# Float32 matmuls of the attention, the scan and the merge, tied together by dependencies

## The chip, the core and the metric

The kernel runs on one core of a Trainium2 chip. The time is that of the device in microseconds (us), from one launch, on data that lies in HBM before it starts. All operands and results are float32.

## The reference, cut to what matters

A decoder block on 256 tokens of width 1024. Two branches read the same normed input: attention with 8 heads of 128 channels (with 256 tokens the block choice leaves plain causal attention), and a state-space branch (S5), a complex diagonal scan over 256 steps with 32 groups of 64 states. The branches are merged by sigmoid gates, and an MLP follows.

```python
h = rms_norm(x, norm_mix_g)
q, k, v, u, g = split(h @ w_in)                  # 3 x 1024, 512, 2 x 1024 columns
o_a = attention(rotary(q), rotary(k), v)         # softmax(q k / sqrt(128), causal) v
o_b = s5_branch(u, ...)                          # y = gelu(C scan(A, B u) + d u); val * sigmoid(gt)
x = x + (sigmoid(g_a) * o_a + sigmoid(g_b) * o_b) @ w_out
h = rms_norm(x, norm_mlp_g)
x = x + square(relu(h @ w_up)) @ w_down
return rms_norm(x, norm_final_g)
```

## The kernel before, in words

**Matmuls.** There are two kinds on TensorE. The large projections are done in float32r: a weight tile of 512 KB is loaded by a DMA on SP's queue, `split` (L82) makes a rounded high part on ScalarE (L83) and the rest on VectorE (L84), and each product is three matmuls, high by high, high by low, low by high (`mm3`, L87 to L90, with 256 moving columns; `tok_mm`, L265 to L269, with 512). The small products inside the branches are plain float32 matmuls, which the profile counts as two passes each, or transposes, one pass each:

- scores of a head, L307 and L310, with two bf16 matmuls that add the causal mask (L309, L312)
- transposes of the probabilities of a head, three at L330, copied to SBUF by ScalarE (L332)
- outputs of a head, L340 and L342, two heads into one PSUM tile `o`, which VectorE reads with the gate into `mixA` (L344)
- the scan: inputs at L539 (weights on 64 rows of the array), and the outputs `y` of a quarter: two matmuls by `Dt` on the whole array (L568) and eight on half the columns of the array, four from `sr` and four from `si` (L574). VectorE makes `sr` at L558 to L560 and `si` at L561 to L563.
- the merge after the gated linear unit: four transposes of a group, two for each half of the tokens (L662).

**Stages.** First `u` and the norm, then the projections `v`, and the four head pairs (q and k at `K`, scores at `S`, the gate at `G`, outputs at `A`) and the four scan quarters (tables `T`, scan `Q`), in the program order of the string `ORDER` (L45). Then the gated linear unit in four groups (L645 to L666), the output projection, the up and the down projection.

**Who sets the order.** The program order is not the order on an engine. A planner goes through the instructions with a simulated clock of its own and puts on each engine, at each moment, the ready instruction of the best priority. Priority is program order, and work inside `tc.high_priority` is moved ahead: the weight splits by 800 places, the scores (`S`) and the transposes and outputs (`A`) by 300 (`ATT_PRIO`). Each engine then runs its list in order, and an instruction whose inputs are late holds all behind it. Tiles come from pools with a fixed number of buffers, and a tile waits until an old one is free: two PSUM banks for scores, transposes, `o` and the merge (`att_bank`, L64), one for `y` (L565), one `sr` and one `si`, two `pr` and `pts`.

The helper `behind` (L95) adds an order without a wait between instructions of one engine. Functions that the change touches, and their callers:

Of the kernel before, what the change touches and what calls it, by code (L numbers as in the profile page):

```python
# [12 lines left out]
AF = mybir.ActivationFunctionType  # L13
ALU = mybir.AluOpType
PSUM = bass.MemoryType.PSUM

P = 128
# [31 lines left out]
def build(ctx, tc, dr, out):  # L49
# [14 lines left out]
    def att_bank(name):  # L64
        return bank("att", 2, name)
# [29 lines left out]
    def behind(ins, others, reason="table set"):  # L95
        for o in others:
            tc.add_manual_dep(ins, o.name, mybir.DependencyInfo(
                mybir.DependencyClass.NoSync, mybir.DependencyReason.DATA), reason=reason)

    def use_set(func):  # L100
        load = S.preload_act_table(func).ins
# [200 lines left out]
    scale = P ** -0.5  # L302
    mixA = p1.tile([P, KD, T], F32, name="mixA")

    def attn_head(q, k, j):
        s = att_bank("s").rearrange("p a b -> p (a b)")
        PE.matmul(s[:, 0:128], q[:, j, 0:128], k[:, j, 0:128], start=True, stop=False,  # L307
                  skip_group_check=True)
        PE.matmul(s[:, 0:128], ident_b, tri_b, start=False, stop=True, skip_group_check=True)  # L309
        PE.matmul(s[:, 128:384], q[:, j, 128:256], k[:, j, :], start=True, stop=False,  # L310
                  skip_group_check=True)
        PE.matmul(s[:, 256:384], ident_b, tri_b, start=False, stop=True, skip_group_check=True)  # L312
        st = p1.tile([P, 6], F32, tag="st", bufs=2, name="st")
        V.tensor_reduce(st[:, 0:1], s[:, 0:128], axis=mybir.AxisListType.X, op=ALU.max)
        V.tensor_reduce(st[:, 1:2], s[:, 128:384], axis=mybir.AxisListType.X, op=ALU.max)
        V.tensor_scalar(st[:, 0:2], st[:, 0:2], -scale, None, op0=ALU.mult)
        pr = p1.tile([P, 384], F32, tag="pr", bufs=2, name="pr")
        act(pr[:, 0:128], s[:, 0:128], AF.Exp, bias=st[:, 0:1], scale=scale,
                     accum_out=st[:, 2:3])
        act(pr[:, 128:384], s[:, 128:384], AF.Exp, bias=st[:, 1:2], scale=scale,  # L320
                     accum_out=st[:, 3:4])
        V.reciprocal(st[:, 4:6], st[:, 2:4])
        S.activation(pr[:, 0:128], pr[:, 0:128], AF.Copy, scale=st[:, 4:5])
        S.activation(pr[:, 128:384], pr[:, 128:384], AF.Copy, scale=st[:, 5:6])
        return pr

    def attn_pt(pr):
        pt = att_bank("pt").rearrange("p a b -> p (a b)")
        for i in range(3):
            PE.transpose(pt[:, i * P : (i + 1) * P], pr[:, i * P : (i + 1) * P], ident)  # L330
        pts = p1.tile([P, 384], F32, tag="pts", bufs=2, name="pts")
        S.copy(pts, pt[:, 0:384])  # L332
        return pts

    def attn_out(hp, prs, tha):
        pts = [attn_pt(x) for x in prs]
        o = att_bank("o")
        for j in range(2):
            hd = 2 * hp + j
            PE.matmul(o[:, j, :], v[:, 0, hd * P : (hd + 1) * P], pts[j][:, 0:256],  # L340
                      start=True, stop=False, skip_group_check=True)
            PE.matmul(o[:, j, 128:256], v[:, 1, hd * P : (hd + 1) * P], pts[j][:, 256:384],  # L342
                      start=False, stop=True, skip_group_check=True)
        V.scalar_tensor_tensor(mixA[:, 2 * hp : 2 * hp + 2, :], tha, 1.0, o,  # L344
                               op0=ALU.add, op1=ALU.mult)

    def gate(first, dst):
        acc = proj_pair(first, "g")
# [181 lines left out]
    def ssm_quad(m):  # L530
# [29 lines left out]
        V.tensor_sub(sr, sr, w)  # L560
        V.tensor_mul(si, b, sn)  # L561
        V.tensor_mul(w, d, cs)
        V.tensor_add(si, si, w)  # L563
        Wr, nWi, Dt = ssm[1:4]
        y = bank("y", 1, "y")  # L565
        for h in range(2):
            p = 2 * m + h
            PE.matmul(y[:, h, 0:P], Dt[:, p, :], U2[:, p, 1 : P + 1], start=(h == 0), stop=False,  # L568
                      skip_group_check=True)
        for i, (w_, s_) in enumerate(((Wr, sr), (nWi, si))):  # L570
            for h in range(2):
                for j in range(2):
                    q = 2 * h + j
                    PE.matmul(y[64 * j : 64 * (j + 1), h, 0:P], w_[:, 4 * m + q, :], s_[:, q, :],  # L574
                              start=False, stop=(i == 1), skip_group_check=True)
        if m < 3:
            S.copy(ysb[:, m], y[:, :, 0:P])
        for q in range(4):
# [66 lines left out]
    for q in range(4):  # L645
        acc = wide_banks(f"glu{q}") if q % 2 else [flat(mm_bank(f"glu{q}{h}")) for h in range(2)]
        for kk_ in range(2):
            wh, wl = w_unit(dr["w_glu"][2 * q + kk_], f"glu{q}{kk_}")
            for k2 in range(2):
                k, w = 2 * kk_ + k2, slice(k2 * 512, (k2 + 1) * 512)  # L650
                for hf in range(2):
                    tok_mm(acc[hf], wh[:, w], wl[:, w], yhl[0][:, 0:4], yhl[0][:, 4:8], k, hf,
                           k == 0, k == 3)
        tp = att_bank(f"mt{q}")
        for hf in range(2):
            sg = p1.tile([P, T], F32, tag=f"ab{hf}", name="sg")
            act(sg, acc[hf][:, 256:512], AF.Tanh, scale=0.5)
            V.scalar_tensor_tensor(sg, sg, 1.0, acc[hf][:, 0:256], op0=ALU.add, op1=ALU.mult)
            tb = thb[q][:, hf, :]
            V.scalar_tensor_tensor(tb, tb, 1.0, sg, op0=ALU.add, op1=ALU.mult)  # L660
            for i in range(2):
                PE.transpose(tp[:, i, hf * P : (hf + 1) * P], tb[:, i * P : (i + 1) * P], ident)  # L662
        two = slice(2 * q, 2 * q + 2)
        V.scalar_tensor_tensor(mixA[:, two, :], tp, 0.5, mixA[:, two, :],
                               op0=ALU.mult, op1=ALU.add)
# [217 lines left out]
```

## Time and profile before

| what | value |
|---|---|
| median of 3 runs | 397.01 us (397.00, 397.01, 402.53) |
| the profiled execution | 397.22 us, its span 395.4 us |
| mean granted TensorE clock | 0.997 of 2.4 GHz |
| ScalarE (ACT) busy | 225.7 us, 57% of the span |
| HBM read, and the rate over the span | 69.18 MB, 178 GB/s |

The span runs from the first to the last instruction on the core, and the time of an execution holds a little more, 1.8 us here. Times of rows are counted from the start of the span. PE is TensorE's matmuls, DVE is VectorE, ACT is ScalarE. A matmul's own duration runs on past the start of the next one, since they are pipelined, so what a matmul costs is read from start to start.

### The profile page before, as it was taken

Reading aid. Unit: us, or ns where it says so; the run is one execution under the profiler, and the core shown is the slowest. Engines: PE = TensorE matmul, PEld = TensorE weight load, DVE = VectorE, ACT = ScalarE, POOL = GpSimd, SP = SyncE. Lnnn points to the kernel's source line nnn. Section 1 sums busy time; section 2 is a strip of 40 time slices with the busy share of each in tenths; the row PEclk is TensorE's granted clock in tenths of the full one; section 3 lists DMA queues with packets and bytes.
Section 4 is the critical chain, followed back from the end, with each engine's and each line's share of the span. In section 5 each row is a group of like instructions: output and inputs, shape, how many; then the busy total and the mean of one; then the engine's idle time right before and its main releaser. Section 6 shows DMA issues by size and latency. Waiting matters only on the chain.

```text
span 395.4 us, 6719 instructions
## 1 busy us (share of the span) xinstructions
PE 385.0 (97%) x2563; PEld 344.5 (87%) x2563; DVE 293.0 (74%) x521; ACT 225.7 (57%) x360; POOL 30.9 (8%) x39
## 2 busy tenths in 40 slices
PE   7999999999999999999999999999999999999993
PEld 4988898989899797888889999999999888888883
DVE  3999999999999997559748686676676444563434
ACT  5867886674466675955636755655556334354313
POOL 4242393000000000000000000000000000000000
PEclk9999999999999999999999999999999999999998
DMA  7995843344625354346486387556565566565202
GB/s 213 389 337 188 251 165 106 108 159 143 220 93 168 107 159 163 111 159 222 153 300 229 109 269 209 180 195 208 179 202 196 183 208 184 188 213 176 92 2 106
DMA packets 23199, 71.57 MB, mean 181 GB/s; under 512 B 2944, under 2 KB 5248, under 8 KB 23168
## 3 DMA queue, kind: packets, MB, share of 16 engines
q1 hardware_dynamic: 20144, 68.92, 53.1%
q10 hardware_dynamic: 3024, 2.23, 1.9%
q8 instruction: 20, 0.33, 0.3%
q14 instruction: 11, 0.09, 0.1%
HBM read 69.18 MB, written 1.05 MB: 178 GB/s over the span
## 4 chain that ended last, share of the span: by engine, by line
PE 86%; DVE 7%; DMA 2%; POOL 1%; issue 1%; ACT 1%; SPq 0%; ACTq 0%
PE up L88 7%; PE up L89 7%; PE up L90 7%; PE dn L736 6%; PE dn L734 6%; PE dn L735 5%; PE u_acc L181 3%; PE gb L269 2%; PE gb L267 2%; PE gb L268 2%; PE glu L269 2%; PE glu L267 2%; PE glu L268 2%; PE wo L268 2%; PE wo L269 2%; PE wo L267 2%
## 5 line engine op out<-in xcount | busy, mean ns | idle before, releaser
L89 PE MATMUL up<-x2l,hi_up 128*128 128x256 f32 x256 | 70.7, 277 | 0.0
L90 PE MATMUL up<-x2h,lo_up 128*128 128x256 f32 x256 | 70.5, 276 | 0.0
L88 PE MATMUL up<-x2h,hi_up 128*128 128x256 f32 x256 | 70.1, 276 | 0.0
L84 DVE TENSOR_TENSOR lo_dn<-raw_dn,hi_dn 128x1024 fp32r<-128x1024 f32 x32 | 39.2, 1225 | 40.4 <-ACT hi_dn L83 40.4
L83 ACT CAST hi_dn<-raw_dn 128x1024 fp32r<-128x1024 f32 x32 | 33.6, 1050 | 49.1 <-PE dn L736 24.6
L84 DVE TENSOR_TENSOR lo_up<-raw_up,hi_up 128x1024 fp32r<-128x1024 f32 x32 | 38.8, 1224 | 23.5 <-ACT hi_up L83 23.5
L83 ACT CAST hi_up<-raw_up 128x1024 fp32r<-128x1024 f32 x32 | 33.3, 1049 | 35.0 <-PE up L89 16.3
L89 PEld LDWEIGHTS up<-x2l,hi_up 128*128 128x128 f32 x256 | 48.1, 188 | 0.0
L90 PEld LDWEIGHTS up<-x2h,lo_up 128*128 128x128 f32 x256 | 48.1, 188 | 0.0
L88 PEld LDWEIGHTS up<-x2h,hi_up 128*128 128x128 f32 x256 | 47.8, 188 | 0.1
L735 PE MATMUL dn<-lo_dn,hh 128*128 128x512 f32 x96 | 37.4, 389 | 0.0
L736 PE MATMUL dn<-hi_dn,hl 128*128 128x512 f32 x96 | 37.4, 389 | 0.0
L734 PE MATMUL dn<-hi_dn,hh 128*128 128x512 f32 x96 | 37.4, 389 | 0.0
L736 PEld LDWEIGHTS dn<-hi_dn,hl 128*128 128x128 f32 x96 | 18.0, 188 | 3.7
L735 PEld LDWEIGHTS dn<-lo_dn,hh 128*128 128x128 f32 x96 | 18.0, 188 | 3.7
L734 PEld LDWEIGHTS dn<-hi_dn,hh 128*128 128x128 f32 x96 | 18.0, 188 | 3.7
L89 PE MATMUL g<-xgl,hi_g 128*128 128x256 f32 x64 | 18.5, 289 | 0.0
L88 PE MATMUL k<-xgh,hi_k 128*128 128x256 f32 x64 | 18.1, 282 | 0.0
L90 PE MATMUL q<-xgh,lo_q 128*128 128x256 f32 x64 | 18.1, 282 | 0.0
L90 PE MATMUL g<-xgh,lo_g 128*128 128x256 f32 x64 | 18.1, 282 | 0.0
L88 PE MATMUL g<-xgh,hi_g 128*128 128x256 f32 x64 | 18.0, 281 | 0.0
L89 PE MATMUL q<-xgl,hi_q 128*128 128x256 f32 x64 | 18.0, 281 | 0.0
(274 smaller groups left out, 1019.6 us busy)
## 6 DMA issues: line engine op xcount, KB each, us to landing
raw_up<-w_up SPq DMA_DIRECT2D x32, 512.0 KB, 4.3
raw_dn<-w_down SPq DMA_DIRECT2D x32, 512.0 KB, 4.3
raw_v<-w_in SPq DMA_DIRECT2D x8, 512.0 KB, 5.5
raw_q<-w_in SPq DMA_DIRECT2D x8, 512.0 KB, 3.3
raw_k<-w_in SPq DMA_DIRECT2D x8, 512.0 KB, 3.2
raw_g<-w_in SPq DMA_DIRECT2D x8, 512.0 KB, 3.8
raw_gb<-w_in SPq DMA_DIRECT2D x8, 512.0 KB, 4.3
raw_glu<-w_glu SPq DMA_DIRECT2D x8, 512.0 KB, 3.3
```

Of the source, the lines that this page charges most:

```text
L83: ins = S.copy(hi, x).ins
L84: V.tensor_sub(lo, x, hi.bitcast(F32))
L88: PE.matmul(o, wh, xh, start=first, stop=False, **kw)
L89: PE.matmul(o, wh, xl, start=False, stop=False, **kw)
L90: PE.matmul(o, wl, xh, start=False, stop=last, **kw)
L181: PE.matmul(u_acc[:, m // 2, m % 2, :], w[:, ws[m]], x[:, k, :], start=(k == 0 and i == 0 and m % 2 == 0), stop=(k == KD - 1 and i == 2), ...
L267: PE.matmul(acc, xh[:, k, rows], wh, start=first, stop=False)
L268: PE.matmul(acc, xh[:, k, rows], wl, start=False, stop=False)
L269: PE.matmul(acc, xl[:, k, rows], wh, start=False, stop=last)
L734: PE.matmul(acc, xh, wh[:, w], start=(k == lead), stop=False, skip_group_check=True)
L735: PE.matmul(acc, xh, wl[:, w], start=False, stop=False, skip_group_check=True)
L736: PE.matmul(acc, xl, wh[:, w], start=False, stop=(k == end), skip_group_check=True)
```

## The change

A second helper, `after`, adds a dependency with a wait. It is used at five places. The first score matmul of a head waits for the VectorE instruction that last read the outputs of the pair before (`left`, L344). The transposes of both heads of a pair wait until the second head's probabilities are scaled (`scaled`, L324). The first output matmul of each head waits for the copies of both heads' transposes (`copied`, L332). All ten `y` matmuls of a scan quarter, the two by `Dt` and the four of `sr` among them, wait for the last VectorE instruction that makes `si` (`done`, L563). The four transposes of a merge group are issued after both halves are merged, and wait for the second half's merge (`merged`, L660). No instruction of an engine is added or taken away other than waits, and what each computes is unchanged.

```diff
+    def after(ins, others, reason):
+        for o in others:
+            tc.add_manual_dep(ins, o.name, mybir.DependencyInfo(
+                mybir.DependencyClass.Sync, mybir.DependencyReason.DATA), reason=reason)
...
+    left, scaled = [], []
     def attn_head(q, k, j):
         s = att_bank("s").rearrange("p a b -> p (a b)")
-        PE.matmul(s[:, 0:128], q[:, j, 0:128], k[:, j, 0:128], start=True, stop=False,
-                  skip_group_check=True)
+        after(PE.matmul(s[:, 0:128], q[:, j, 0:128], k[:, j, 0:128], start=True, stop=False,
+                         skip_group_check=True).ins, left[-1:], "a pair's scores together")
...
-        S.activation(pr[:, 128:384], pr[:, 128:384], AF.Copy, scale=st[:, 5:6])
+        scaled.append(S.activation(pr[:, 128:384], pr[:, 128:384], AF.Copy, scale=st[:, 5:6]).ins)
         return pr
-    def attn_pt(pr):
+    def attn_pt(pr, last):
         pt = att_bank("pt").rearrange("p a b -> p (a b)")
         for i in range(3):
-            PE.transpose(pt[:, i * P : (i + 1) * P], pr[:, i * P : (i + 1) * P], ident)
+            after(PE.transpose(pt[:, i * P : (i + 1) * P], pr[:, i * P : (i + 1) * P], ident).ins,
+                   [last], "a pair's transposes together")
         pts = p1.tile([P, 384], F32, tag="pts", bufs=2, name="pts")
-        S.copy(pts, pt[:, 0:384])
+        copied.append(S.copy(pts, pt[:, 0:384]).ins)
         return pts
+    copied = []
     def attn_out(hp, prs, tha):
-        pts = [attn_pt(x) for x in prs]
+        last = scaled[2 * hp + 1]
+        pts = [attn_pt(x, last) for x in prs]
         o = att_bank("o")
         for j in range(2):
             hd = 2 * hp + j
-            PE.matmul(o[:, j, :], v[:, 0, hd * P : (hd + 1) * P], pts[j][:, 0:256],
-                      start=True, stop=False, skip_group_check=True)
+            after(PE.matmul(o[:, j, :], v[:, 0, hd * P : (hd + 1) * P], pts[j][:, 0:256],
+                             start=True, stop=False, skip_group_check=True).ins,
+                   copied[-1:], "a pair's outputs together")
...
-        V.scalar_tensor_tensor(mixA[:, 2 * hp : 2 * hp + 2, :], tha, 1.0, o,
-                               op0=ALU.add, op1=ALU.mult)
+        left.append(V.scalar_tensor_tensor(mixA[:, 2 * hp : 2 * hp + 2, :], tha, 1.0, o,
+                                           op0=ALU.add, op1=ALU.mult).ins)
...
-        V.tensor_add(si, si, w)
+        done = V.tensor_add(si, si, w).ins
...
-            PE.matmul(y[:, h, 0:P], Dt[:, p, :], U2[:, p, 1 : P + 1], start=(h == 0), stop=False,
-                      skip_group_check=True)
+            after(PE.matmul(y[:, h, 0:P], Dt[:, p, :], U2[:, p, 1 : P + 1], start=(h == 0),
+                             stop=False, skip_group_check=True).ins, [done], "y together")
...
-                    PE.matmul(y[64 * j : 64 * (j + 1), h, 0:P], w_[:, 4 * m + q, :], s_[:, q, :],
-                              start=False, stop=(i == 1), skip_group_check=True)
+                    after(PE.matmul(y[64 * j : 64 * (j + 1), h, 0:P], w_[:, 4 * m + q, :],
+                                     s_[:, q, :], start=False, stop=(i == 1),
+                                     skip_group_check=True).ins, [done], "y together")
...
+        tbs = []
         for hf in range(2):
...
-            V.scalar_tensor_tensor(tb, tb, 1.0, sg, op0=ALU.add, op1=ALU.mult)
+            merged = V.scalar_tensor_tensor(tb, tb, 1.0, sg, op0=ALU.add, op1=ALU.mult).ins
+            tbs.append(tb)
+        for hf in range(2):
             for i in range(2):
-                PE.transpose(tp[:, i, hf * P : (hf + 1) * P], tb[:, i * P : (i + 1) * P], ident)
+                after(PE.transpose(tp[:, i, hf * P : (hf + 1) * P],
+                                    tbs[hf][:, i * P : (i + 1) * P], ident).ins,
+                       [merged], "a group's transposes together")
```

## Rows read from the trace of the kernel before

**Rows 1.** The page: busy time, share, instructions; then the last chain by engine.

```profile
PE 385.0 (97%) x2563; PEld 344.5 (87%) x2563; DVE 293.0 (74%) x521; ACT 225.7 (57%) x360; POOL 30.9 (8%) x39
...
PE 86%; DVE 7%; DMA 2%; POOL 1%; issue 1%; ACT 1%; SPq 0%; ACTq 0%
```

**Rows 2.** Windows: stretch, length; PE, PEld, DVE, ACT, POOL busy us (instructions); clock, DMA.

```profile
66.00:90.00 24.00, 23.44 (x202) 21.77 (x202) 24.00 (x47) 16.41 (x29) 0.00 (x0) 1.00 0.37 121
```

**Rows 3.** Waits of TensorE: waiting line, releaser, us in total, times, longest.

```profile
PE s L307 <- DVE k L299: 0.7, 1, 0.7
...
PE pt L330 <- ACT pr L323: 0.5, 1, 0.5
```

**Rows 4.** Timeline of TensorE, one transpose among float32r matmuls: start, us, what.

```profile
119.84 0.28 PE L88 MATMUL g<-xgh,hi_g 128*128 128x256 f32 x1
119.96 0.27 PE L330 MATMUL pt<-cst,pr 128*128 128x128 f32 x1
119.99 0.36 PE L89 MATMUL g<-xgl,hi_g 128*128 128x256 f32 x1
120.19 0.28 PE L90 MATMUL g<-xgh,lo_g 128*128 128x256 f32 x1
```

**Rows 5.** Timeline of TensorE, half of a scan quarter's outputs among float32r matmuls.

```profile
89.34 0.28 PE L90 MATMUL k<-xgh,lo_k 128*128 128x256 f32 x1
89.55 0.66 PE L574 MATMUL y<-si,nWi 128*64 128x128 f32 x8
90.14 0.38 PE L88 MATMUL k<-xgh,hi_k 128*128 128x256 f32 x1
90.36 0.28 PE L89 MATMUL k<-xgl,hi_k 128*128 128x256 f32 x1
```

**Rows 6.** Timeline of TensorE, the other places of L574 and what splits them.

```profile
82.70 0.44 PE L574 MATMUL y<-sr,Wr 128*64 128x128 f32 x4
83.07 0.44 PE L330 MATMUL pt<-cst,pr 128*128 128x128 f32 x2
83.44 0.44 PE L574 MATMUL y<-sr,Wr 128*64 128x128 f32 x4
...
103.29 0.28 PE L90 MATMUL k<-xgh,lo_k 128*128 128x256 f32 x1
103.50 0.48 PE L539 MATMUL x<-U,W 64*128 64x128 f32 x2
103.91 0.66 PE L574 MATMUL y<-si,nWi 128*64 128x128 f32 x8
104.50 1.16 PE L539 MATMUL x<-U,W 64*128 64x128 f32 x14
...
105.81 0.28 PE L89 MATMUL q<-xgl,hi_q 128*128 128x256 f32 x1
...
148.65 0.43 PE L574 MATMUL y<-sr,Wr 128*64 128x128 f32 x2
...
153.41 0.66 PE L574 MATMUL y<-si,nWi 128*64 128x128 f32 x8
```

**Rows 7.** Timeline of TensorE, a stall at transposes, and later attention work.

```profile
79.63 0.33 PE L330 MATMUL pt<-cst,pr 128*128 128x128 f32 x1 [0.49 <-ACT pr L323]
...
82.50 0.27 PE L330 MATMUL pt<-cst,pr 128*128 128x128 f32 x1
...
154.00 0.49 PE L307 MATMUL s<-k,q 128*128 128x128 f32 x2
```

**Rows 8.** Timeline of ACT: the second head's scaling of the first pair.

```profile
81.33 0.50 ACT L324 ACTIVATE pr<-pr,st 128x256 f32<-128x256 f32 x1
```

**Rows 9.** Timeline of DVE: the end of `si` twice, and a pair's outputs.

```profile
87.97 0.68 DVE L563 TENSOR_TENSOR si<-si,sw__748 128x512 f32<-128x512 f32 x1
...
149.63 0.67 DVE L563 TENSOR_TENSOR si<-si,sw__1854 128x512 f32<-128x512 f32 x1
150.23 0.67 DVE L344 SCALAR_TENSOR_TENSOR mixA<-tha,o 128x512 f32<-128x512 f32 x1
```

## The prediction, made before the changed kernel was run

> **What bounds the kernel now.** I read the busy times of the page first, then the chain that ended last, the windows of the attention stage, the list of TensorE's waits, and at the end TensorE's timeline around each small float32 product. TensorE's matmuls cover 97% of the span, and 86% of the last chain is TensorE's [rows 1]. The 97% overstates how well it is used, since a matmul's recorded time runs into the next one, but it says that TensorE hardly ever stands still. VectorE is the other full engine in the stage that the change touches: 24.00 of 24 us from 66 to 90 us, with TensorE at 23.44 [rows 2]. Yet TensorE waited for it or for ScalarE only twice in this stage, 0.7 us for the first pair's keys and 0.5 us for the first pair's probabilities [rows 3]. So time saved on TensorE's list of work is time saved at the end, as long as the other two still deliver before TensorE asks. The change adds and removes no work on any engine. It only moves instructions on TensorE's list, and so its price is in the seams between kinds of matmul and in waits.
>
> **A seam at the full array costs nothing.** Take one transpose alone among float32r matmuls [rows 4]. From the start of the L88 before it to the start of the second matmul after it is 120.19 - 119.84 = 0.35 us, which holds that L88, the transpose and one L89. A float32r matmul of this shape is 0.12 us from start to start (119.84 to 119.96), so the transpose is charged 0.35 - 0.24 = 0.11 us. Its neighbour looks slow (119.99 to 120.19 is 0.20 us) only because the transpose looks short (0.03 us). In the middle of a run a pass of this size also takes 0.11 us, since even two transposes with a tiled product before and behind them take no more than 83.44 - 83.07 = 0.37 us [rows 6]: 0.22 for the two and 0.15 at the borders of the tiled product. So gathering transposes (L330, L662), scores (L307, L310) and attention outputs (L340, L342), all full array, is worth 0.00 to 0.01 us for each seam removed. I count 19 such seams less (ten of transposes, four of outputs, two of scores, three of the merge): 0 to 0.2 us, taken as 0.1.
>
> **A seam at the tiled products costs 0.35 us.** The eight L574 matmuls of a quarter use half of the array's columns. One visit of eight passes [rows 5]: from the L90 before (89.34) to the second matmul after it (90.36) is 1.02 us, less 0.23 for the two float32r matmuls gives 0.79 us. Inside, eight passes take 90.14 - 89.55 = 0.59 us and four take 83.07 - 82.70 = 0.37 us [rows 5, 6], so two passes more cost 0.11 us. Four times 0.11 is work; the other 0.35 us is the seam, paid once for each visit whatever its length.
>
> The Trainium skill (TensorEngine Tiling (Array Packing), Key Properties) says that a change of tiling mode, not just of tile, drains TensorE. By that rule, too, only the L574 part of this change can gain, and the change from L568 to L574 inside the new block drains once as before; a reading in which each float32 visit costs something has no support there. The trace agrees with it: 0.35 us at the tiled seam against 0.01 at the other.
>
> **The sum of the y blocks.** Now the eight matmuls, 16 passes, of each quarter come in pieces: I count ten over the four quarters, six of them in [rows 5, 6], the others like them. The first quarter has three (82.70 and 83.44, split by transposes, and 89.55), the last three, the others two each. After the change there are four, one per quarter: six seams less, 6 x 0.35 = 2.1 us. Two of the ten pieces lie inside the input matmuls L539, which are tiled another way. The whole stretch there is 105.81 - 103.29 = 2.52 us, less 0.23 is 2.29 [rows 6]. L539 alone, 16 passes, would take 8 x 0.11 + 0.35 = 1.23 and L574 alone 0.79, together 2.02; the nesting costs 0.2 to 0.3 more. If the block lies clear of L539, two of these go: 0.4 us. L568's four passes cost 0.11 us each wherever they stand. From the y blocks thus 2.5 us; the bounds are 0 (every block is broken again) and 2.7.
>
> **The stall at the first transposes.** TensorE stood 0.49 us at 79.63 until the first head's probabilities were scaled [rows 7]. After the change these transposes stand behind the second head's scaling, which ended at 81.33 + 0.50 = 81.83, where the first of the second head's transposes ran at 82.50, 0.67 us later [rows 7, 8]. So the stall goes, 0.5 us. It can come back in the new place, since the saved time itself brings TensorE there 0.5 us earlier and leaves 0.2 us of the 0.67. Bounds: gain 0.5, nothing, or a wait of 0.5 as now; I take the gain. The 0.7 us stall at the keys is before any of the new waits and stays. It could grow by 0.4 us, because two seams of the first quarter's L568 that fill time before it move away; the planner puts other matmuls there, so I take 0.
>
> **The new waits.** Each waits for the same engine that the instruction waited for already, only for a later instruction of it, so I count no wait instructions. Behind each stands all of TensorE's list. The cover is that TensorE comes late to these places now. The last part of `si` ended at 88.65 and 150.30 [rows 9], and TensorE came to the matmuls that need it at 89.55 and 153.41 [rows 5, 6], 0.9 and 3.1 us later. The pair's outputs were read at 150.23 + 0.67 = 150.90 [rows 9], and the second head's scores of the next pair began at 154.00 [rows 7], 3.1 us later. The first head's scores now wait for the same read, but the second head's need not wait for a later bank any more, so the pair ends no later. What comes later is `y` itself, by about 1 us in each quarter (L568 and the `sr` half now stand in front of the `si` half): its copy on ScalarE and, for three quarters, the 24 small DMAs on ScalarE's queue, none needed before the gelu; and the next quarter's `sr`, which has one buffer and so waits for the block on VectorE. If this cover is gone, a place costs what such waits cost now, 0.5 to 0.7 us [rows 3]. SP's weight loads and POOL are not passed by anything; I put them at 0.
>
> **What the dependency does not do.** Work of the attention has 300 places of priority and may still break into a y block. It did so in two of the eight half-blocks (82.70 to 83.44 and at 148.65) [rows 6]. I take one break in the four new blocks: -0.35 us.
>
> **The sum.** 2.5 + 0.1 + 0.5 - 0.35 = 2.75 us, off the profiled execution's 397.22 us: 394.5. The profile was 0.2 us over the median of the runs, so 394.3 us for the median; forecast, **394.3 us**, 0.7% less.
>
> **Rival 1: no visible gain.** The attention breaks the blocks again: six breaks at 0.35 us eat 2.1 of the 2.5 us, the stall at the transposes stays, 397.0 - 0.5 = 396.5 us. For it: two breaks out of eight halves now. Against: a block lasts only some 1.7 us, and the wait makes its ten matmuls ready at one moment.
>
> **Rival 2: slower, the held blocks stall TensorE.** Fifteen blocks of the attention and the scan now begin with a wait (three pairs' scores, four of transposes, four of outputs, four y). The planner's clock is not the chip's; where VectorE, full from 66 to 90 us [rows 2], or ScalarE is later than planned, the whole list of TensorE stands, at 0.6 us a place. It decides from the sixth late block on (6 x 0.6 = 3.6 over the gain of 2.75 to 3.1). With ten of fifteen: 397.0 - 2.75 + 6.0 = 400.3 us. For it: both waits of now are of this kind [rows 3], and a gain brings TensorE earlier everywhere. Against: the slack of 0.67 to 3.1 us above.
>
> **Rival 3: every float32 visit costs.** If the 0.20 us after a transpose were a price of its own, 0.09 us over a matmul, the 19 full-array seams would be worth 1.7 us, 392.6 us. Against it stand [rows 4], which give the time back in the transpose.
>
> **How the numbers follow.** Chances: forecast 0.55, rival 1 0.22, rival 2 0.17, rival 3 0.06. The forecast's own bounds are 393.5 (no break, and the nesting and seams at their highest) to 395.5 (two more breaks, one late block). For 8 in 10 the range goes down to rival 3 and up through rival 1 to the mild half of rival 2, where eight blocks are late: 392.2 to 398.4. Two per cent, about what a measurement of this kernel can tell from no change, is 7.9 us. Faster than 389.1 would need more than all seams and stalls together (2.7 + 0.2 + 1.2 = 4.1): 0.01. Slower than 405.0 needs 18 late blocks of 0.6 us, more than there are, or one long one: 0.03. Within: 0.96.
>
> **What would show it.** In the timeline after: four pieces of L574, each of 16 passes with L568's four in front; a whole block, from the last float32r matmul before to the second after it, less two, at 4 x 0.11 + 8 x 0.11 + 0.35 = 1.67 us; transposes in sixes, scores of both heads side by side; no wait of 0.49 us at L330; TensorE's list of waits with nothing new over 0.7 us; and the first L734 of the down projection some 2.5 us earlier. Wrong would be: blocks still in more than six pieces (rival 1), new entries of L307, L330, L340 or L568 in the waits that sum to more than 3 us (rival 2), or a gain that lies where only transposes were gathered, after 165 us (rival 3).

## The result, and the profile after

The kernel takes **408.18 us** after the change (median of 6 runs, 406.88 to 409.02) against 397.0 us before (median of 6). One of those six runs took 402.53 us and the others 396.1 to 398.4, so versions are compared by their medians. The ratio is 1.027, 95% interval 1.024 to 1.030: slower, by four times the gain that was forecast and outside the range. The profiled execution took 408.04 us, its span is 406.2 us, 10.8 more than before.

First the page of the changed kernel: busy times, TensorE, ScalarE and the granted clock in 40 slices of 10.2 us, and the chain by engine.

```profile
PE 385.4 (95%) x2563; PEld 346.2 (85%) x2563; DVE 292.6 (72%) x521; ACT 225.9 (56%) x360; POOL 29.3 (7%) x39
...
PE   7999999999999989389999999999999999999993
...
ACT  6867977565564374644554675556555433453323
...
PEclk8999999999999999779999999999999999999998
...
PE 70%; DVE 14%; ACT 5%; issue 4%; DMA 4%; POOL 2%; ACTq 1%; SPq 0%; DVEq 0%
```

The work is the same as in [rows 1], TensorE's busy time within 0.4 us. Nearly all of the loss is in one place: the 17th slice (162.5 to 172.6 us) has a 3 for TensorE, and the clock falls to 7 in it and in the next. Stages bear that out. From the first scores to the first matmul of the gated linear unit (`glu`, L272) took 165.66 - 66.08 = 99.6 us before and 175.11 - 65.77 = 109.3 us after, 9.8 more; `glu` to output projection took 1.1 more; all later stages together are within 0.3 us.

TensorE's waits of the changed kernel (line, releaser, us in total, times, longest); this answers [rows 3].

```profile
PE pt L337 <- ACT pr L331: 8.7, 2, 8.3
PE gb L272 <- ACT thb L112: 1.4, 1, 1.4
...
PE s L314 <- ACT cs L534: 0.8, 1, 0.8
PE gb L272 <- DVE q L302: 0.7, 1, 0.7
```

One wait of 8.3 us for the scaling of probabilities is nearly all of it. TensorE's timeline after: the first pair's transposes, a whole `y` block, and the big wait.

```profile
82.62 0.88 PE L337 MATMUL pt<-cst,pr 128*128 128x128 f32 x6 [0.38 <-ACT pr L331]
...
108.92 0.28 PE L90 MATMUL q<-xgh,lo_q 128*128 128x256 f32 x1
109.04 0.61 PE L580 MATMUL y<-U,Dt 128*128 128x128 f32 x4
109.58 0.66 PE L586 MATMUL y<-sr,Wr 128*64 128x128 f32 x8
110.06 0.61 PE L586 MATMUL y<-si,nWi 128*64 128x128 f32 x8
110.60 0.39 PE L88 MATMUL q<-xgh,hi_q 128*128 128x256 f32 x1
110.82 0.28 PE L89 MATMUL q<-xgl,hi_q 128*128 128x256 f32 x1
...
163.72 0.38 PE L314 MATMUL s<-k,q 128*128 128x128 f32 x2
...
165.35 0.22 PE L319 MATMUL s<-tri_b,ident_b 128*128 128x128 bf16 x1
173.92 1.54 PE L337 MATMUL pt<-cst,pr 128*128 128x128 f32 x6 [8.35 <-ACT pr L331]
175.11 0.78 PE L272 MATMUL glu<-hi_glu,yhl 128*128 128x512 f32 x1
...
176.11 0.63 PE L272 MATMUL glu<-hi_glu,yhl 128*128 128x512 f32 x1
176.54 0.63 PE L273 MATMUL glu<-lo_glu,yhl 128*128 128x512 f32 x1
```

The last pair's scores stand at the very end of TensorE's list before `glu`, at 163.72; before, the second head's began at 154.00 [rows 7], and projection matmuls of `gb` filled the time behind them. What ScalarE does in the 8.35 us:

```profile
167.83 0.48 ACT L112 ACTIVATE pr<-s,st 128x256 f32<-128x256 f32 x1
...
168.42 1.28 ACT L106 ACT_TABLE_LOAD   x1
169.71 0.42 ACT L112 ACTIVATE yT<-yT 128x256 f32<-128x256 f32 x1
...
170.72 1.01 ACT L112 ACTIVATE yT<-yT 128x256 f32<-128x256 f32 x3
171.64 1.54 ACT L112 ACTIVATE thb<-gb,rs_half 128x256 f32<-128x256 f32 x4
...
173.36 0.51 ACT L331 ACTIVATE pr<-pr,st 128x256 f32<-128x256 f32 x1
173.76 0.46 ACT L83 CAST yhl<-yT 128x256 fp32r<-128x256 f32 x1
```

Read it from below. `glu` needs `yhl`, which is made from the gelu of `yT`; the gelu needs another table set of ScalarE, loaded in 1.28 us; and that load comes, in ScalarE's order, behind the last exponential of the last pair's softmax. So the scan's result and the last pair's transposes both stand behind the last scores. The Trainium skill (ScalarE: Activation LUTs, What ACT_TABLE_LOAD costs) gives about 1283 ns for the load, and about 2.66 us for a whole switch of sets with a drain behind the load. The row agrees with the first, 1.28 us; of the second nothing is seen here, since the gelu starts at 169.71, 0.01 us behind the load.

Windows of the changed kernel (stretch, length; PE, PEld, DVE, ACT, POOL busy; clock, DMA share, rate):

```profile
66.00:90.00 24.00, 23.62 (x203) 22.67 (x203) 24.00 (x47) 17.16 (x30) 0.00 (x0) 1.00 0.40 130
...
173.90:178.00 4.10, 4.08 (x13) 3.50 (x14) 1.52 (x4) 2.16 (x6) 0.00 (x0) 0.50 0.00 0
```

The first line answers [rows 2] and hardly differs. In the second the granted clock is 0.50, the 1.2 GHz level, right behind the 8.35 us without matmuls, and `glu` matmuls are 0.43 us apart (176.11 to 176.54) instead of 0.23; that is the 1.1 us lost inside `glu`.

### The profile page after: what moved, and what is told of

Its sections match the earlier page's. It is cut to its first block, busy times and chain, and to the rows that moved or that the text cites. A ratio compares the mean times of both kernels' runs of the same rounds, so it can differ in the third digit from the quotient of the medians.

```text
span 406.2 us, 6710 instructions
## 1 busy us (share of the span) xinstructions
PE 385.4 (95%) x2563; PEld 346.2 (85%) x2563; DVE 292.6 (72%) x521; ACT 225.9 (56%) x360; POOL 29.3 (7%) x39
## 4 chain that ended last, share of the span: by engine, by line
PE 70%; DVE 14%; ACT 5%; issue 4%; DMA 4%; POOL 2%; ACTq 1%; SPq 0%; DVEq 0%
PE up L88 7%; PE up L90 7%; PE up L89 7%; PE dn L754 5%; PE dn L753 5%; PE dn L752 5%; PE glu L272 2%; PE glu L273 2%; PE glu L274 2%; PE wo L272 2%; PE wo L273 2%; PE wo L274 2%; DMA raw_v<-w_in 2%; DVE lo_g L84 1%; PE dnw L754 1%
## 5 line engine op out<-in xcount | busy, mean ns | idle before, releaser
L84 DVE TENSOR_TENSOR lo_glu<-raw_glu,hi_glu 128x1024 fp32r<-128x1024 f32 x8 | 9.8, 1223 | 13.0 <-ACT hi_glu L83 13.0
L88 PE MATMUL q<-xgh,hi_q 128*128 128x256 f32 x64 | 18.2, 284 | 0.0
L89 PE MATMUL k<-xgl,hi_k 128*128 128x256 f32 x64 | 18.0, 281 | 0.0
```

The lines of the kernel that those rows point to most:

```text
L84: V.tensor_sub(lo, x, hi.bitcast(F32))
L88: PE.matmul(o, wh, xh, start=first, stop=False, **kw)
L89: PE.matmul(o, wh, xl, start=False, stop=False, **kw)
```

## The experiments

The theory that came out of these rows: the dependencies themselves cost little, but with them the planner makes another list, in which the last pair is late, and the junction "last softmax, table load, gelu, `glu`" pays for it. Rivals: one single dependency is to blame; the loss is a sum of many small waits; or something behind `glu`. All ratios are to runs of the kernel before that were measured beside the version, with medians of 396.9 to 397.5 us; a trace is of one execution. In the diffs, taking a dependency out of the changed kernel leaves an empty list in its place.

### Which part carries the loss

**The changed kernel without the scores' wait.**

```diff
-                         skip_group_check=True).ins, left[-1:], "a pair's scores together")
+                         skip_group_check=True).ins, [], "a pair's scores together")
```

> The changed kernel without the scores' wait for the read of the pair before; the other four waits stay. Theory A (that wait puts the pairs in series, the last pair comes after TensorE's other work has run out, and the 8.35 us stall at L337 with the half clock behind it is the loss): the last pair's first head is scored right behind the outputs of the pair before, the stall shrinks to under 3 us, the time comes back to 397 to 401 us. Theory B (holding y for the last part of si delays the scan and, over its one buffer of sr, the attention's VectorE work): no more than 2 us come back, 406 to 408 us. Theory C (the held transposes and outputs delay the pairs): also 405 to 408 us.

Measured 403.5 us, ratio 1.016 [1.013, 1.020]; `glu` at 171.22, wait at L337 6.7 us. Theory A asked for 397 to 401 us and so holds in part: the loss falls from 11.2 to 6.0 us, and the wait for the read of the pair before carries about 5 us of it, not all.

**The kernel before with the scores' wait alone.**

```diff
-        PE.matmul(s[:, 0:128], q[:, j, 0:128], k[:, j, 0:128], start=True, stop=False,
-                  skip_group_check=True)
+        after(PE.matmul(s[:, 0:128], q[:, j, 0:128], k[:, j, 0:128], start=True, stop=False,
+                         skip_group_check=True).ins, left[-1:], "a pair's scores together")
```

> The kernel before with the scores' wait alone. Theory A: slower by most of the loss, 404 to 408 us, with a stall of 5 us or more at the last pair's transposes. Theories B and C: 396 to 399 us.

Measured 404.14 us, 1.017 [1.014, 1.019], in theory A's range; `glu` at 170.09. TensorE has no long wait in it, but three of 1.0 to 1.5 us at the last pair's transposes and one of 0.6 at `glu`, and behind them the granted clock is 0.50 from 170.1 to 176 us.

**The kernel before with `y` together alone.** The attention and the merge are as before.

```diff
+            after(PE.matmul(y[:, h, 0:P], Dt[:, p, :], U2[:, p, 1 : P + 1], start=(h == 0),
+                             stop=False, skip_group_check=True).ins, [done], "y together")
...
+                    after(PE.matmul(y[64 * j : 64 * (j + 1), h, 0:P], w_[:, 4 * m + q, :],
+                                     s_[:, q, :], start=False, stop=(i == 1),
+                                     skip_group_check=True).ins, [done], "y together")
```

> The kernel before with the scan quarter's ten matmuls held together, nothing else. Theory A: the six tiled seams less show as a gain, 394 to 397 us, no new stall before the gated linear unit. Theory B: 403 us or more, with the stall before the gated linear unit. Theory C: as A.

Measured 404.37 us, 1.017 [1.015, 1.019], as theory B had it; so A and B both hold a part. This run says most about the mechanism, since no attention instruction has a new wait in it. TensorE's timeline of it:

```profile
159.79 0.39 PE L314 MATMUL s<-k,q 128*128 128x128 f32 x2
...
163.88 0.38 PE L314 MATMUL s<-k,q 128*128 128x128 f32 x2
...
171.12 0.47 PE L337 MATMUL pt<-cst,pr 128*128 128x128 f32 x1 [5.92 <-ACT pr L330]
...
172.95 0.78 PE L272 MATMUL glu<-hi_glu,yhl 128*128 128x512 f32 x1
```

The last pair's scores are 10 us later than before (159.79 and 163.88 against 149.77 and 154.00 [rows 7]), and TensorE did not wait for them: it had 35 instructions between 159 and 165 and was never idle there. They stand later in its list. Between 118 and 140 us VectorE, full all the time, ran 4 softmax and 19 scan instructions, where the kernel before ran 9 and 15. So with `y` held until `si` is made, more of the scan's VectorE work stands ahead of the softmax in the planner's order; why the planner does so is not shown.

**The changed kernel without `y` together.**

```diff
-                             stop=False, skip_group_check=True).ins, [done], "y together")
+                             stop=False, skip_group_check=True).ins, [], "y together")
...
-                                     skip_group_check=True).ins, [done], "y together")
+                                     skip_group_check=True).ins, [], "y together")
```

> The changed kernel without the y block (its ten matmuls are free again), the other four waits stay. Theory A: still slow, 405 to 410 us, since the scores' wait is in it. Theory B: 397 to 400 us. Theory C: 405 to 408 us.

Measured 406.84 us, 1.023 [1.020, 1.026]; L337 waits 8.1 us.

**Transposes, outputs and merge together, scores and `y` not held** (both edits above).

> The changed kernel without the scores' wait and without the y blocks: the transposes, outputs and merges held alone. If the loss comes from the scores' wait and the y blocks: 396 to 399 us. If any hold in the chain of pairs makes the last pair late, as its slack before was about 2 us: 399 to 404 us with a stall of 2 us or more before the gated linear unit.

Measured 403.11 us, 1.015 [1.013, 1.017]: any hold in the chain of pairs makes the last pair late.

**Transposes and outputs together alone**, and **the merge together alone**, each on the kernel before.

```diff
+                   [last], "a pair's transposes together")
...
+                   copied[-1:], "a pair's outputs together")
```

> The kernel before with a pair's transposes together and its outputs together, nothing else of the change. Together with the merge they gave 403.1, 5.7 us over before. Theory F: the last pair's transposes now wait for the second head's scaling, all three parts of the attention's end stand in one piece before the gated linear unit (glu at 169 to 170), 402 to 404 us, so that these two dependencies carry all of the loss of that run and the merge none. Rival: the merge carries it, and this one is 396 to 399.

```diff
+        for hf in range(2):
+            for i in range(2):
+                after(PE.transpose(tp[:, i, hf * P : (hf + 1) * P],
+                                    tbs[hf][:, i * P : (i + 1) * P], ident).ins,
+                       [merged], "a group's transposes together")
```

> The kernel before with the merge group's transposes held together and nothing else of the change. Up to the gated linear unit nothing is touched, and there the planner gives the same list as before. Theory F: glu at 165.5 to 166.0, 396 to 398 us, the same as before; the part is free, as predicted (0 to 0.1 us). Rival: each held group waits for its second half, 0.6 us a place, 398 to 400 us.

The first measured 403.36 us, 1.018 [1.014, 1.022], `glu` at 169.18, with these waits in the stage:

```profile
PE pt L337 <- ACT pr L331: 3.4, 1, 3.4
...
PE glu L272 <- ACT yhl L83: 1.1, 1, 1.1
```

The second measured 396.76 us, 0.998 [0.995, 1.001]. So the merge is free, as predicted, and each of the three other parts alone costs 6.0 to 6.8 us. They don't add up (19.5 us alone, 11.2 together): all are paid at the same junction, as waits before `glu` and as half clock behind them. Up to `glu` the scores' wait alone takes 5.1 us more than before, `y` 7.0 and the transposes and outputs 3.9; from `glu` to the output projection it is 2.8, 0.3 and 2.6 more; behind that all three are within 0.2 us of before. It can be read in one table. "Scaled" is the end of the last pair's scaling.

| kernel | last pair's scores | scaled | `glu` starts |
|---|---|---|---|
| before | 149.8, 154.0 | 162.0 | 165.66 |
| changed | 163.7, 164.5 | 173.9 | 175.11 |
| scores' wait alone | 158.1, 158.9 | 169.0 | 170.09 |
| `y` alone | 159.8, 163.9 | 171.5 | 172.95 |
| transposes, outputs alone | 153.6, 159.1 | 167.1 | 169.18 |

In the kernel before (ScalarE's row first, then TensorE's):

```profile
161.52 0.49 ACT L324 ACTIVATE pr<-pr,st 128x256 f32<-128x256 f32 x1
```

```profile
165.19 0.40 PE L269 MATMUL gb<-hi_gb,xgl 128*128 128x512 f32 x1
165.42 0.49 PE L330 MATMUL pt<-cst,pr 128*128 128x128 f32 x3
165.66 0.47 PE L267 MATMUL glu<-hi_glu,yhl 128*128 128x512 f32 x1
```

There `glu` came 3.7 us after the scaling, since `gb` matmuls filled TensorE until 165.42; in the four slower ones it comes 1.1 to 2.1 us after it. The last pair had 3.4 us of slack (162.0 to 165.42), and the held versions make it 5 to 12 us later.

### Is it the table load?

**The changed kernel with the gelu ahead of the last pair.** `X` loads a table set, `Y` is the gelu; a load more, and the last scores no longer stand before the gelu.

```diff
-         "B0 G3 S3 X1 Y0 A3 B1")
+         "B0 X1 Y0 X0 G3 S3 A3 B1")
```

> The changed kernel, all five waits, with the gelu of the scan's output put ahead of the last pair's softmax in program order (and the softmax's table set loaded once more, 1.28 us on ScalarE). Theory A1 (the gated linear unit waits, over ScalarE's table set, for the last pair's softmax, and the last pair is late by what the new waits add to the chain of pairs): TensorE runs the gated linear unit while the last pair is worked off, the 8 us stall and the half clock behind it go, 395 to 399 us. Theory A2 (TensorE stands because the last pair's transposes are ahead of the gated linear unit in its list, whatever ScalarE does): the stall stays, 404 us or more.

The same order was put into the kernel before as control, into the version with `y` alone, and into the changed kernel without the scores' wait.

> The kernel before with the same order: the control. TensorE has no stall before the gated linear unit there, so theory A1 gives 396 to 399 us, no gain and at most the price of one more table load; if the order itself is worth something whatever the waits, it is under 395.

> The y blocks alone, with the order of the run before this. Theory A1: the six tiled seams less, 2.5 us, show at last against the control with the same order: 393 to 396 us. If the y blocks cost the time in another way (over the one buffer of sr, say), it is over 399.

> The changed kernel without the scores' wait, with the same order. Theory A1: 394 to 397 us, the same as the changed kernel with this order within 1.5 us, since the pairs' lateness no longer meets TensorE's end of work.

Measured: 404.45 us, 1.019 [1.014, 1.024]; control 397.28, 1.000 [0.998, 1.001]; `y` alone 403.89, 1.017 [1.013, 1.020]; without the scores' wait 402.5, 1.012 [1.006, 1.018]. Only the control came as expected; the three others took 5.5 to 7.9 us more than the most that theory A1 allowed. The mechanism of the stall is shown: the wait before `glu` is gone in all of them, and `glu` starts at 163.87, 164.55, 162.47 and 163.05, earlier than in the kernel before (in part only because 6 to 22 matmuls of the last pair now come behind its first). But the time is lost again further on: from the first output-projection matmul to the end the three take 4.7, 6.4 and 3.6 us more than the kernel before, the control 0.4. (The trace of the last is of its fastest execution, 399.33 us; the median lies 3.2 us above it.) Waits of the version with `y` alone:

```profile
PE up L89 <- DVE x2l L710: 2.4, 1, 2.4
PE xt L705 <- DVE x2t L703: 1.3, 1, 1.3
```

This is a second junction. `x2t`, the reload of `x` for the MLP (1 MB), takes the memory of the first stage, so SP issues it only when the last merge's last split is done; it lands 7 to 10 us later, and the residual sum, the transposes `xt` and the up projection hang on it. SP's rows of it, issue time first, in the kernel before and in this version:

```profile
200.13 0.39 SPq L672 DMA_DIRECT2D x2t<-x  x1
```

```profile
204.79 0.39 SPq L685 DMA_DIRECT2D x2t<-x  x1
```

Counted from the first output-projection matmul, the issue comes 9.9 us later before (190.19) and in the control (189.52 to 199.46), but 13.0, 14.9 and 13.6 us later in the three others. Yet TensorE stood for the reload itself only once, the 1.3 us at `xt` above; in each of the three it had landed 2.5 to 4.7 us before the up projection began. What sets them apart is TensorE's list. Between the first `xt` and the up projection stand eight output-projection matmuls in the kernel before and in the control, eight or ten in all other versions, and none in these three and in the first version of the next part. Nothing there covers the way from `xt` over ScalarE and VectorE to `x2l`, which the up projection needs. That the late reload made the planner order it so is not shown. In the kernel before (TensorE's rows, then VectorE's):

```profile
210.91 1.03 PE L692 MATMUL xt<-cst,x2t 128*128 128x128 f32 x8
211.70 0.48 PE L268 MATMUL wo<-lo_wo,mxh 128*128 128x512 f32 x1
...
213.61 0.40 PE L88 MATMUL up<-x2h,hi_up 128*128 128x256 f32 x2
```

```profile
213.27 0.87 DVE L697 SCALAR_TENSOR_TENSOR x2l<-xt,par,x2h 128x256 fp32r<-128x256 f32 x2
```

### Is the seams' gain real, and where does it go?

**`y` together alone, with the attention's priority at 900 places instead of 300**, so that the planner puts the softmax ahead again; **the kernel before** and **the changed kernel** with the same priority.

```diff
-ATT_PRIO = 300
+ATT_PRIO = 900
```

> The y blocks alone, with the priority of scores, transposes and outputs raised from 300 to 900 places. Theory D (VectorE is full until 130 us and the y blocks cost time only because the planner then puts the scan's VectorE work ahead of the softmax of the third and fourth pair, so that the last pair ends after TensorE's other work): the last pair's scaling ends by 164 us, no stall over 1 us before the gated linear unit, and the tiled seams less show as a gain: 393.5 to 396 us, 1 to 3.5 under the kernel before. Theory E (the y blocks themselves hold up the scan, over one buffer of sr and of y, whatever the priority): the last scaling stays at 170 us or later, 402 to 405 us.

> The kernel before with the same priority, the control: no stall to take away there, 396 to 398 us by both theories. Under 395 the priority alone would be worth what the run with the y blocks gains.

> The changed kernel, all five waits, with the priority of 900. Theory D: the y block's part of the lateness goes, the scores' wait keeps its own (alone it cost 6.6 us): 400 to 405 us, a stall of 3 to 6 us at the last pair's transposes. Theory E: 406 to 409 us as without it.

Measured: 402.16 us (399.9 to 405.41), 1.012 [1.008, 1.016]; 401.79, 1.012 [1.009, 1.015]; 404.54, 1.018 [1.017, 1.020]. The time expected of the first was missed by 6 us. The control was missed as well: both theories had it at 396 to 398 us, and the priority alone costs 4.4 us. In it the last pair is scaled at 166.5, 4.5 us later than before, TensorE waits 1.7 us for it and 0.8 us at `glu`, and the half clock follows. So more priority does not simply put the softmax ahead; what it does hangs on the rest of the list. The third came out in the range of theory D, with a longer wait at the last pair's transposes than it gave (7.5 us for 3 to 6). In the first, theory D's mechanism is half there: the last pair is scaled at 160.6, `glu` at 163.27 and the output projection at 187.78, both 2.4 us earlier than before, which is the size predicted for the seams. Then the second junction takes it (TensorE's timeline, VectorE's, then windows, as above):

```profile
210.32 1.03 PE L705 MATMUL xt<-cst,x2t 128*128 128x128 f32 x8
212.00 0.50 PE L88 MATMUL up<-x2h,hi_up 128*128 128x256 f32 x2 [0.64 <-ACT x2h L709]
215.36 0.58 PE L89 MATMUL up<-x2l,hi_up 128*128 128x256 f32 x1 [2.86 <-DVE x2l L710]
```

```profile
214.83 0.87 DVE L710 SCALAR_TENSOR_TENSOR x2l<-xt,par,x2h 128x256 fp32r<-128x256 f32 x2
```

```profile
212.00:216.00 4.00, 1.14 (x5) 0.93 (x6) 3.87 (x8) 2.79 (x6) 0.00 (x0) 0.79 0.79 243
216.00:220.00 4.00, 4.00 (x20) 4.00 (x20) 1.52 (x4) 1.40 (x4) 0.00 (x0) 0.50 0.46 151
```

The reload had landed at 208.90, and TensorE came to `xt` at 210.32 without a wait. But `x2l` comes 4.5 us behind the start of `xt` instead of 2.4, since three splits and, other than before, the next two residual sums stand ahead of it in VectorE's list from 210.23 on; and no output-projection matmul covers that time. The first 48 up matmuls took 12.37 us instead of 6.53 (waits, then half clock): 5.8 us. The other 3.2 us of this stage come from up matmuls 0.118 us apart instead of 0.113, all through the stage. Why is open, but it does not come from the waits: the same spacing stands in one other trace, the control without `y` further down, where the stage has no wait and a granted clock of 1.00, and in none of the other eighteen. The profiled execution here took 404.66 us, 2.5 over the median. The reload's issue came 12.5 us behind the output projection's start (200.30 against 187.78).

**`y` and merge together, priority 900.** With the merge held, too, the planner puts eight output-projection matmuls behind the second half's `xt` transposes, as in the kernel before.

```diff
-ATT_PRIO = 300
+ATT_PRIO = 900
...
+            after(PE.matmul(y[:, h, 0:P], Dt[:, p, :], U2[:, p, 1 : P + 1], start=(h == 0),
+                             stop=False, skip_group_check=True).ins, [done], "y together")
...
+                after(PE.transpose(tp[:, i, hf * P : (hf + 1) * P],
+                                    tbs[hf][:, i * P : (i + 1) * P], ident).ins,
+                       [merged], "a group's transposes together")
```

> The y matmuls together and a merge group's transposes together, nothing else of the change, with the attention's priority at 900 places. With y alone at 900 the gated linear unit and the output projection began 2.4 us earlier than in the kernel before, and the time was lost behind them, where the reload for the MLP came late to TensorE (2.9 and 0.6 us of waits at L710 and half clock). With the merge held together too the planner puts eight output-projection matmuls behind the second token half's transposes again, as in the kernel before. Theory F, two junctions where TensorE is served just in time (the last pair's softmax before the gated linear unit, and the last merge and reload before the up projection): glu at 163 to 164, wo at 187.5 to 189, no wait over 1 us before up, 393.5 to 396 us. Rival G, the loss behind wo in the run with y alone was of another kind (up matmuls at 0.118 instead of 0.113 us, whatever the reload does): up starts by 213 but down starts no earlier than 307, 400 us or more. Rival H, the planner's placing is not kept on the chip and the first junction stalls again: glu after 166, 400 to 404.

Measured **394.4 us** (393.65 to 394.59), 0.992 [0.991, 0.994]: 2.9 us under the kernel before, clear of the noise. `glu` at 162.28, output projection at 186.52, reload issued 9.9 us after that. Its waits from 66 us on, and its clock by slices:

```profile
PE up L89 <- DVE x2l L715: 0.7, 1, 0.7
...
PE pt L337 <- ACT pr L330: 0.5, 1, 0.5
```

```profile
PEclk9999999999999999999999999999999999999999
```

From first scores to `glu` it takes 162.28 - 65.23 = 97.05 us, 2.5 less than before. In both kernels this stretch holds 754 matmuls of TensorE, with 1.3 us of idle time here and 1.2 before, all at the full clock; what differs is the visits of L574 (here L586), four here and ten before, and those of L539, three and five. So the time is that of the seams. With `y` alone at 900 the stretch was as short, 97.14 us. All four `y` blocks are whole in it (the `Dt` matmuls, eight passes and eight passes side by side, from 89.08, 105.50, 132.48 and 150.87). Here the predicted 2.5 us stand at the end of the kernel. Without the merge it was the 402.16 us above. Three more runs ask for the other edits: **priority 600** instead of 900, **without `y`**, and **without the priority**.

> As the one before with the attention's priority at 600 places. The last pair's transposes then stand behind 7 instead of 12 matmuls of the gb projection at the end of TensorE's list before the gated linear unit. Theory F: the same 393.5 to 397, at most 1 us more than with 900, as the wait for the last scaling at L331 grows by up to 5 matmuls of 0.23 us. Rival G: 400 or more, down starts after 307. Rival H: glu after 166, 400 to 404.

> The kernel before with the merge's transposes together and the attention's priority at 900 places, y not held: the control of the fastest version (394.4 us), which also holds y. The planner leaves one matmul of the gb projection in front of the last pair's transposes, as in the control without the merge (401.8 us). Theory F: glu at 167.5 to 168, 400 to 402.5 us, so that priority and merge alone gain nothing, and the fastest version needs the y blocks. Rival: priority and merge carry the gain, 393.5 to 396 us.

> The y matmuls together and the merge's transposes together at the attention's priority of the kernel before, 300 places. The last pair's scores stand at the end of the gb projection's list as with y alone (404.4 us). Theory F: glu at 171 to 173.5, 402.5 to 405.5 us, so that the fastest version needs the attention's priority as well. Rival: the merge mends it without the priority, 394 to 398 us.

Measured 396.07 us, 0.997 [0.996, 0.998] (`glu` at 163.89); 402.3, 1.011 [1.007, 1.015] (`glu` at 167.61); 404.57, 1.019 [1.017, 1.021] (`glu` at 171.66). So the gain needs all three edits, and less priority gives less of it: 1.7 us more than with 900 places, where at most 1 was expected (98.18 us from first scores to `glu`, with 1.6 us idle; the rest of the difference is open). The last two lie where the theory of the two junctions had them, in time and at `glu`. For the one without `y` that is partly luck: its trace is of its slowest execution, 403.99 us, and 3.3 of the 6.8 us by which it exceeds the trace of the kernel before are up matmuls 0.118 us apart, which the theory did not have. The rival that the loss behind the output projection is of another kind holds for these 3.2 and 3.3 us. The version of 394.4 us lost 0.8 us in that stage, 0.7 of it a wait, and its up matmuls are 0.113 us apart.

## Why the prediction was wrong

- **What bounds the kernel.** TensorE's list did bound the kernel before, but only "as long as the other two still deliver before TensorE asks". That clause was measured where TensorE then stood, and never at the junction from 157 to 166 us, where ScalarE's table load, gelu and casts lie between the last softmax and `glu`.
- **The seam.** Right: a whole `y` block is 110.82 - 108.92 - 0.23 = 1.67 us, as predicted. The changed kernel has six pieces, not five as taken: scores break the third block at 135.73, transposes the last at 155.18. Where the blocks are whole and nothing else is late, the stretch is 2.5 us shorter, the predicted term (97.05 and 97.14 us against 99.6; 98.18 with less priority).
- **The first transposes.** The stall came back in the new place, one of the bounds: 0.38 us idle at 82.62, against 0.49 at 79.63 [rows 7].
- **The new waits, taken as nothing: the step that failed.** It said "The first head's scores now wait for the same read, but the second head's need not wait for a later bank any more, so the pair ends no later." The last pair ends 12 us later. The slack at each place was read from the old list, 3.1 us for these scores, as if the rest of the list stayed. And it was read at the second head's scores, 154.00 [rows 7]; the first head's, which got the wait, began at 149.77 in the kernel before, 1.1 us before that read ended at 150.90, so they had no slack even in the old list. In the new list the outputs of the second pair end at about 127 us, and VectorE reads them at 132.41, the scores that wait for that read come at 135.73, and at the last pair the delay is 10 to 14 us. Even `y` alone, which adds no wait to the attention, moves the last pair by 10 us. Slack in a planned list is no property of a place.
- **Rival 2** had the sign and not the mechanism. There are no ten late blocks at 0.6 us; there is one wait of 8.35 us, three of 0.4, 0.7 and 1.4, and 1.1 us of half clock. Its sign of being wrong, new waits of over 3 us in sum, came at L337 (L330 before), 8.7 us. The 0.03 for "one long one" was the case that came.
- **Rivals 1 and 3** fell: neither broken blocks (four of six seams are gone, 1.4 of 2.1 us by the price above) nor any gain from full-array products was seen.
- **Left at nothing and rightly so:** the merge alone (0.998), SP and POOL in this change, which no wait of TensorE behind 66 us names. The reload on SP's queue held up TensorE once, for 1.3 us, in a version without the first stall.

What stays open: why the planner's list with `y` held puts the scan's VectorE work ahead is shown by counts, not by its costs; why priority alone makes the last pair late; and the up matmuls at 0.118 us in two traces.

## What to carry to other kernels

Where a planner writes the engines' lists, a dependency is an input to the planner: price it by the new list, or ask of every junction where two chains meet (here the softmax and the scan before `glu`, the reload and the output projection before the up projection) how late its last input may come, and which work covers the way. A saved seam shows at the end only if those junctions stay in time; look there first, and try to mend the list before giving up the edit. That is a search and no rule: the priority that helped here cost the kernel before 4.4 us. Parts that each lose 6 to 7 us alone and 11 together point to one shared place, not to the parts.

## What the runs showed of the hardware

In the changed kernel the granted clock fell to 0.50, the 1.2 GHz level, in the wait of 8.35 us without matmuls and was still there from 173.9 to 178 us. Shorter waits did it, too: with `y` alone and more priority, one of 2.86 us behind one of 0.64 (0.50 from 216 to 220 us); in the kernel before with more priority, one of 1.7 and one of 0.8 us (0.51 from 167.8 to 174), and `glu` to the output projection took 2.8 us longer. In the changed kernel without the scores' wait and with the gelu first, waits of 0.6 and 1.9 us were followed by 1.00 (213.5 to 222 us). So with small waits the half clock can cost as much as the waits. The Trainium skill (TensorE: Matmul & The Clock Gate, HAM oscillation) describes a loss behind waits for DMAs that adds to the wait. The trace agrees for a wait for ScalarE: in the changed kernel it was 1.1 us inside `glu` on top of 8.35.
